# A hybrid state-space and convolution block on one core: a convolution split by parity, statistics and loads in another order, other paces

## The chip, the cores and the metric

The kernel runs on 1 core of one Trainium2 chip. The metric is device time in microseconds; before the change the median of 3 runs is 3039.42 us (3037.2 to 3045.06).

## The reference

One transformer-like block on x of 2048 tokens by 1024 channels, in float32. Cut to what matters:

```python
mod = silu(c) @ w_mod + b_mod                        # shifts, scales and gains, 6 x 1024
h = modulate(rmsnorm(x + pos), sh1, sc1)
p = h @ w_in                                         # 512 | 1024 | 1024 | 1024 | 1024 columns
y = s5_bidirectional(p[:, :512], context, ...)       # two linear scans over time
ya = gelu(y + d * u); ya = ya * sigmoid(ya @ w_glu)
vb = p[:, 512:1536] * sigmoid(p[:, 1536:2560])
vb = depthwise_conv(vb, dw_kernel, taps=31, padding=15) + dw_bias
vb = silu(layernorm(vb))
merged = sigmoid(g_a) * (ya @ w_proj_a) + sigmoid(g_b) * (vb @ w_proj_b)
x = x + g1 * (merged @ w_out)
x = x + g2 * (silu(h2 @ w_gate) * (h2 @ w_up)) @ w_down
return rmsnorm(x)
```

## The kernel before

Activations lie channel-major: a tile is 128 channels by 1024 tokens, and tokens go in two halves of 1024. Each matmul operand is split into a high and a low part (`split`, lines 192 to 196; weights in `wload`, lines 152 to 165), and each product is three matmuls of 128x128 by 512 columns: high by high, high by low, low by high. Everything larger than the on-chip memory goes through DRAM tensors whose names begin with `d_`.

The kernel is written as a foreground of matmul loops and a background of generators. After every three matmuls of a k step, `tick()` (lines 80 to 86) adds `RATE` credits, and background generators, in the order of their list, are stepped while the credit is positive; a generator yields what its step costs in credits, or a tuple with a number of ticks to wait. `dve()` takes credits off for VectorE's work in the foreground. `finish()` empties a generator at once. This sets the program order; each engine works its own queue in order, the building layer moves an instruction forward where its operands are ready, `high_priority()` moves it further, and `behind(ins, LAG)` ties a convolution pass to the LAG-th instruction before it on its engine.

The stages, in order, with the lines that the change and the steps touch:

- **Start** (`run`, lines 1547 to 1609). `mod_load` issues the loads of w_mod on SyncE's queue; `loads(k)` puts the load of x tile k-1 between them and, at the end, two weight tiles. `mod_first` multiplies c by w_mod; inside it `vectors()` (line 244) loads the small vectors and dw_kernel on ScalarE's queue and transposes them, and `stats(k)` takes the row statistics of x tiles 0 to 3 at k = 2 and of tiles 4 to 7 at k = 4 (`norm_stat`). Then `norm_first` turns, scales and splits the first 512 tokens of h, and `v_first` (line 860) makes the first gated tile of the convolution's input, four groups of 24 matmuls.
- **Projections, half 0** (lines 1632 to 1668): `v_pair`, `u` and `g_tile` (gate tiles d_g). In the background `build_prep` (line 468) and `build` prepare the state-space matrices, and `convolve` runs the convolution of half 0.
- **Convolution** (`conv`, line 904): for each of 8 channel tiles, a load of 1054 (or 1039) columns into a `cin` tile (2 buffers), a first product on ScalarE (line 917) into an `acc` tile (3 buffers, shared with others), 30 passes of multiply and add over the whole width on VectorE (line 919), a running sum over tiles (line 924), and a store of `acc` to d_cv on the POOL queue (line 925). `conv_edge` does the 15 columns at the seam; `conv_stat` takes mean and variance, `conv_apply` normalizes.
- **State-space stage** (lines 1676 to 1684), beside `v_pair` and 14 gate tiles of half 1.
- **Tail** (`tail`, line 1703). `stage_b` (line 975) is the gated branch: 4 preparing steps (yah, yal), 4 GLU tiles that end in zah and zal, 8 tiles of w_proj_a. Its two halves b0 and b1 come one after the other, with `chain` (conv_apply, then mod_rest and the convolution of half 1) in the background. `merge`, `out_proj` and the feed-forward part `ffn_s` follow for half 0, then the same for half 1. In `feed` (line 1739) `h2s_first`, `h2s_second` and `sums` prepare operands beside `out_proj` and the first four FFN products (lines 1369 to 1383); `weights_open` takes one `acc` and other tiles as weight buffers.

Of the kernel before, what the change touches and what calls it, by code (L numbers as in the profile page):

```python
# [19 lines left out]
N = 2048  # L20
# [8 lines left out]
RATE = (0.75, 0.7, 0.66, 0.61, 0.6, 0.9)  # L29
CREDIT = 3.0  # L30

W_BUILD, W_NORM, W_MOD = 4, 4, 20
W_IN, W_SWAP, W_OUT = 2, 6, 2
W_SUM = 4
LAG = 4

G_EARLY = 14
# [3 lines left out]
GAP_L, GAP_R = 1184, 2016  # L41


class Kernel:
# [146 lines left out]

    def split(self, full, hi, lo):
# [11 lines left out]
    def setup(self):  # L204
# [15 lines left out]
        self.d_vp = dt([8, 128, N], "d_vp")  # L220
# [23 lines left out]
    def vectors(self):  # L244
        nc, A, cp = self.nc, self.A, self.cp
        rows = self.t4(shape=(88, 128), name="vrows")
        r = 0
        self.vcol = {}
        for name in ("b_mod", "norm1_g", "norm2_g", "dw_bias", "conv_norm_g", "conv_norm_b"):
# [4 lines left out]
            r += n  # L254
        ps = self.ms([128, 88])
        nc.tensor.transpose(ps, rows, self.ident[0:88, 0:88])
# [4 lines left out]
        dwr = self.t4(shape=(31, 1024), name="dwr")  # L261
        nc.scalar.dma_start(dwr, A["dw_kernel"][0])
        ps = self.ms([128, 8, 31])
        for k in range(8):
            nc.tensor.transpose(ps[:, k, :], dwr[:, k * 128 : (k + 1) * 128], self.ident[0:31, 0:31])
        nc.vector.tensor_copy(self.dwk, ps)

# [3 lines left out]
        self.s2 = cp.tile([128, 8], F32, name="s2")  # L271

# [195 lines left out]
    def build_prep(self, bp, xq):  # L468
# [18 lines left out]
        Ct = bp.tile([128, 2, 32, 16], F32, name="Ct")  # L487
        for r, nme in enumerate(("ssm_c_re", "ssm_c_im")):
            Cr = xq("Craw", F32, (128, 4, 2, 64))
            for d in range(2):  # L490
# [5 lines left out]
            ps = self.ms([128, 512])  # L496
            for q in range(4):
                nc.tensor.transpose(ps[:, q * 128 : (q + 1) * 128], Cr[:, q].rearrange("k g p -> k (g p)"), self.ident)
            v.tensor_copy(Ct[:, r].rearrange("p a c -> p (a c)"), ps)
            yield (0,)  # L500
# [120 lines left out]
        Br = xq("Braw", F32, (128, 2, 32, 16))  # L621
        Bt = bp.tile([128, 2, 32, 16], F32, name="Bt")
        for r, nme in enumerate(("ssm_b_re", "ssm_b_im")):
            nc.scalar.dma_start(Br[:, r], A[nme][0].rearrange("d (r g) p c -> (g p) (d r) c", g=2))
# [235 lines left out]
    def v_first(self, ws):  # L860

        nc = self.nc
        ps = [self.mm(), self.mm()]
        for b in range(2):
            for p, w in zip(ps, ws):
                self.gemm(p, w, 0, *self.h[0], blocks=(b,))
# [962 lines left out]
```

## Time and profile before

| what | us |
|---|---|
| median of 3 runs | 3039.42 |
| the profiled execution | 3042.31 |
| its span, first to last instruction | 3040.5 |
| TensorE (PE) busy | 2890.9 |
| VectorE (DVE) busy | 2182.9 |
| ScalarE (ACT) busy | 1221.0 |
| mean granted TensorE clock | 0.975 |

The profile is one execution. A page gives busy times; other views of the same trace give groups of instructions, waits, a timeline, and busy times in chosen stretches. "PE" is TensorE, "DVE" VectorE, "ACT" ScalarE, "SP" SyncE; a "q" behind the name is the engine's queue of instructions that issue DMA. An idle time is put down to what ended it last.

### The profile page before, as it was taken

The numbers are of one execution on the slowest core, as the hardware profiler recorded it, in microseconds if no ns is written. First come the engines' busy times: TensorE is split into PE (matmuls) and PEld (weight loads), VectorE is DVE, ScalarE is ACT, GpSimd is POOL, SyncE is SP. The second block draws the span as 40 slices with busy tenths as digits, with TensorE's granted clock in tenths as the row PEclk, the third lists the DMA queues.
The fourth block names the chain that finished last, engine by engine and source line by source line (L and its number), as shares of the span: only waits on it lengthen the run. The fifth ranks groups of instructions, "written<-read, shape, count | busy, mean of one in ns | idle before, by whom it ended". The sixth has DMA issues, their size and how long they took to land. (4 is left out here: it accounts for less than half of the span.)

```text
span 3040.5 us, 34659 instructions
## 1 busy us (share of the span) xinstructions
PE 2890.9 (95%) x12747; PEld 2335.4 (77%) x12747; DVE 2182.9 (72%) x3296; ACT 1221.0 (40%) x1675; POOL 313.2 (10%) x480
## 2 busy tenths in 40 slices
PE   7989999998999989998899999989999899999998
PEld 3768777777888767876677887868787788888887
DVE  6489988899899477896878897866466744344446
ACT  4323344334343472123534444445324544444443
POOL 0111311100011000000000011000100000110110
PEclk9999999999999999999999999999999999999999
DMA  5344544533443566856554566463756544664553
GB/s 202 124 116 126 155 158 159 166 110 110 124 127 101 180 208 236 279 171 204 117 123 114 127 142 141 115 163 110 203 199 215 133 106 111 138 136 111 113 122 130
DMA packets 400009, 450.09 MB, mean 148 GB/s; under 512 B 34849, under 2 KB 318849, under 8 KB 399840
## 3 DMA queue, kind: packets, MB, share of 16 engines
q1 hardware_dynamic: 336224, 272.59, 28.9%
q0 software_dynamic: 50160, 170.55, 23.0%
q10 hardware_dynamic: 13456, 4.75, 0.7%
q8 instruction: 100, 1.64, 0.2%
q14 instruction: 69, 0.57, 0.1%
HBM read 280.42 MB, written 167.36 MB: 147 GB/s over the span
## 5 line engine op out<-in xcount | busy, mean ns | idle before, releaser
L919 DVE SCALAR_TENSOR_TENSOR acc<-cin,dwk,acc 128x1009 f32<-128x1009 f32 (+1 forms) x480 | 609.5, 1272 | 3.8
L183 PE MATMUL mm<-hh,hi 128*128 128x512 f32 x1152 | 480.6, 417 | 1.8 <-ACT hi L161 1.3
L183 PE MATMUL mm<-hh,lo 128*128 128x512 f32 x1152 | 457.2, 397 | 0.8 <-DVE lo L163 0.8
L183 PE MATMUL mm<-hl,hi 128*128 128x512 f32 x1152 | 456.4, 396 | 0.0
L1215 PE MATMUL mm<-ah,hi 128*128 128x512 f32 x704 | 277.1, 394 | 16.8 <-DVE fg L1380 13.5
L1215 PE MATMUL mm<-ah,lo 128*128 128x512 f32 x704 | 275.4, 392 | 3.4 <-DVE lo L1249 3.4
L161 ACT ACTIVATE hi<-raw 128x1024 fp32r<-128x1024 f32 x148 | 156.2, 1055 | 286.4 <-PE mm L183 249.2
L1215 PE MATMUL mm<-al,hi 128*128 128x512 f32 x704 | 267.9, 393 | 0.0
L183 PEld LDWEIGHTS mm<-hh,lo 128*128 128x128 f32 x1152 | 219.0, 190 | 49.8 <-DVE lo L163 1.7
L183 PEld LDWEIGHTS mm<-hh,hi 128*128 128x128 f32 x1152 | 219.8, 191 | 48.6 <-issue 2.2
L183 PEld LDWEIGHTS mm<-hl,hi 128*128 128x128 f32 x1152 | 219.8, 191 | 44.8 <-issue 0.6
L1457 POOL DMA_DIRECT2D d_x<-fd x152 | 129.1, 851 | 1069.1 <-ACT fd L1456 1063.3
L163 DVE TENSOR_TENSOR lo<-raw,hi 128x1024 fp32r<-128x1024 f32 x148 | 180.5, 1220 | 79.4 <-ACT hi L161 76.5
L1456 ACT ACTIVATE fd<-mm,mod 128x1024 f32<-128x1024 f32 x152 | 166.9, 1111 | 134.5 <-PE mm L1215 102.2
L1249 DVE TENSOR_TENSOR lo<-raw,hi 128x1024 fp32r<-128x1024 f32 x85 | 103.8, 1221 | 131.8 <-ACT hi L1246 130.5
L1249 DVE TENSOR_TENSOR lo<-ex,hi 128x1024 fp32r<-128x1024 f32 x83 | 101.4, 1221 | 108.0 <-ACT hi L1246 107.7
L1215 PEld LDWEIGHTS mm<-ah,hi 128*128 128x128 f32 x704 | 133.5, 190 | 47.5 <-DVE fg L1380 14.8
L1215 PEld LDWEIGHTS mm<-ah,lo 128*128 128x128 f32 x704 | 133.2, 189 | 32.5 <-DVE lo L1249 4.9
L1303 ACT ACTIVATE fg<-fg 128x512 f32<-128x512 f32 x80 | 50.6, 632 | 265.0 <-DVE fg L1306 265.0
L1215 PEld LDWEIGHTS mm<-al,hi 128*128 128x128 f32 x704 | 133.4, 190 | 28.0 <-issue 0.5
L183 PE MATMUL mm<-mgh,hi 128*128 128x512 f32 x256 | 101.4, 397 | 4.3 <-ACT mgh L195 2.0
L1215 PE MATMUL mm<-B22h,ex 128*128 128x512 f32 x320 | 105.3, 390 | 0.0
(490 smaller groups left out, 6146.3 us busy)
## 6 DMA issues: line engine op xcount, KB each, us to landing
d_x<-fd POOLq DMA_DIRECT2D x152, 512.0 KB, 9.2
raw<-in_w_in_dram SPq DMA_DIRECT2D x72, 512.0 KB
wm<-in_w_mod_dram SPq DMA_DIRECT2D x48, 512.0 KB
d_g<-gsig POOLq DMA_DIRECT2D x32, 512.0 KB, 4.0
raw<-in_w_out_dram SPq DMA_DIRECT2D x32, 512.0 KB
raw<-in_w_ffn_up_dram SPq DMA_DIRECT2D x28, 512.0 KB
raw<-in_w_ffn_down_dram SPq DMA_DIRECT2D x25, 512.0 KB
ex<-in_w_ffn_down_dram SPq DMA_DIRECT2D x23, 512.0 KB
```

The source lines that it names most:

```text
L161: nc.scalar.activation(hi, raw, AF.Copy)
L163: nc.vector.tensor_tensor(lo, raw, hi.bitcast(F32), op=OP.subtract)
L183: nc.tensor.matmul(ps[:, b * bw : (b + 1) * bw], wt[:, k, c0 : c0 + 128], mv[k][:, b * bw : (b + 1) * bw], start=(k == 0 and j == 0), stop ...
L919: self.behind(nc.vector.scalar_tensor_tensor(a, x[:, i : i + W], K(i), a, op0=OP.mult, op1=OP.add), LAG)
L1215: nc.tensor.matmul(ps, wt[:, k, c0 : c0 + 128], mv[k], start=start and k == 0 and j == passes[0], stop=stop and k == n - 1 and j == passes ...
L1249: i = nc.vector.tensor_tensor(lo, f, hi.bitcast(F32), op=OP.subtract)
L1303: self.last_act = nc.scalar.activation(o, i, f)
L1456: nc.scalar.activation(o, ps, AF.Copy, scale=mod)
L1457: nc.gpsimd.dma_start(self.d_x1[r, :, hs], o, accum_op=OP.add)
```

## The change

Numbers: `RATE` goes from (0.75, 0.7, 0.66, 0.61, 0.6, 0.9) to (0.75, 0.65, 0.61, 0.61, 0.6, 0.64), `W_MOD` from 20 to 12, `G_EARLY` from 14 to 12, and an unused gap of on-chip memory shrinks.

**Convolution.** The input d_vp is stored as even and odd columns apart (`[8, 128, 2, N // 2]`). With E and O the even and odd columns, one filter of 16 taps goes over E, one of 15 over O, and one of 16 taps (the pairwise sums of the taps, `dws`) over E + O; even outputs are the third less the first two, odd outputs the sum of the first two. Each runs over 512 columns. The results lie in the `cin` tile and are stored from there; half 1 keeps two fixed accumulators. The order of tokens in d_cv is by parity, and `merge` undoes it.

```diff
-        a = vp.tile([128, HALF], F32, tag="acc", name=self.nm("acc"), bufs=3)[:, 0:W]
+        a, b = accs or [vp.tile([128, HALF], F32, tag="acc", name=self.nm("acc"), bufs=3) for _ in range(2)]
+        p1, p2, q = a[:, 0:512], a[:, 512:1024], b[:, 0:512]
         K = lambda i: self.dwk[:, ft, i : i + 1]
-        nc.scalar.activation(a, x[:, 0:W], AF.Identity, scale=K(0), bias=self.V("dw_bias", ft))
-        for i in range(1, 31):
-            self.behind(nc.vector.scalar_tensor_tensor(a, x[:, i : i + W], K(i), a, op0=OP.mult, op1=OP.add), LAG)
-            yield 1.18
+        o = 1 if hf else 0
+        TS(p1, E[:, 0:512], K(0), None, op0=OP.mult)
+        TS(p2, O[:, o : o + 512], K(1), None, op0=OP.mult)
+        yield 0.8
+        for j in range(1, 16):
+            self.behind(STT(p1, E[:, j : j + 512], K(2 * j), p1, op0=OP.mult, op1=OP.add), LAG)
+            if j < 15:
+                self.behind(STT(p2, O[:, j + o : j + o + 512], K(2 * j + 1), p2, op0=OP.mult, op1=OP.add), LAG)
+            yield 1.2
+        TT(E, E, O, op=OP.add)
+        TS(q, E[:, 0:512], self.dws[:, ft, 0:1], None, op0=OP.mult)
+        yield 1.0
+        for j in range(1, 16):
+            self.behind(STT(q, E[:, j : j + 512], self.dws[:, ft, j : j + 1], q, op0=OP.mult, op1=OP.add), LAG)
+            yield 0.6
...
+        STT(q, q, bias, p1, op0=OP.add, op1=OP.subtract)
+        if hf == 0:
+            TT(ye, q, p2, op=OP.subtract)
+            STT(yo[:, 0:511], p1[:, 0:511], bias, p2[:, 1:512], op0=OP.add, op1=OP.add)
...
+        yield 1.8
...
-        nc.gpsimd.dma_start(self.d_cv[ft, :, hf * HALF : hf * HALF + W], a)
+        nc.gpsimd.dma_start(self.d_cv[ft, :, hf * HALF : (hf + 1) * HALF], y)
         yield 1.2
```

`conv_edge` takes 16 columns instead of 15 and writes them by parity. In `conv_stat` two loads of d_cv go ahead, half 1 waits six ticks before each step, and half 1 uses the convolution's two accumulators as mean and variance.

**Start.** `vectors_load()` issues the small vectors before `mod_load`; dw_kernel comes last on SyncE's queue and its transposes (`taps()`) after `v_first`; statistics of x tiles 4 to 7 leave `mod_first`, and `v_first`, now a generator over k with both weight tiles at each step, runs interleaved with `norm_first` and those statistics.

```diff
                 def loads(k):
                     if k == 8:
                         wr.extend(self.wraw(w) for w in wsrc)
-                    if k:
+                        self.norm_load(x, xt[4:8], nc.sync)
+                        self.dwr = self.t4(shape=(31, 1024), name="dwr")
+                        nc.sync.dma_start(self.dwr, A["dw_kernel"][0])
+                    elif 0 < k < 5:
                         self.norm_load(x, xt[k - 1 : k], nc.sync)
...
+                go = self.v_first(ws)
+                for k in range(8):
+                    for _ in range(5 if k == 0 else 2):
+                        next(first, None)
+                    next(second_stat, None)
+                    next(go)
```

In `build_prep` the loads of B follow those of C at once, and the transposes of C come after the scalar chain.

**Products.** `gemm_pair` works two output tiles together, all k steps but the last first; `stage_b` uses it for its first two w_proj_a tiles and `out_proj` for the first two of the first 512 tokens. In `ffn_s` the activation, product and split of the first four tiles get high priority.

```diff
+    def gemm_pair(self, pair, mhi, mlo, blocks=(0, 1)):
+        nc = self.nc
+        kt = len(mhi)
+        for ks in (range(kt - 1), (kt - 1,)):
+            for ps, (whi, wlo), c0 in pair:
+                for b in blocks:
+                    bs = slice(b * 512, (b + 1) * 512)
+                    for k in ks:
+                        for j, (wt, mv) in enumerate(((whi, mhi), (whi, mlo), (wlo, mhi))):
+                            nc.tensor.matmul(
...
```

**Gate tiles.** Tiles 12 and 13 of half 1 come beside b0's preparation, 14 and 15 in `tail`; the chain waits for the second.

```diff
         def chain(cv):
-            while cv in self.bgq:
+            while cv in self.bgq or not gates:
                 yield (2,)
...
         take(b0, 4)
+        self.g_tile(14, (1,))
         b1 = self.stage_b(1, "P", "P")
         e = self.bg(self.prep_b(b1))
         take(b0)
         self.finish(e)
+        take(b1, 4)
+        self.g_tile(15, (1,))
+        gates.append(True)
         take(b1)
```

## Rows read from the trace of the kernel before

**Rows 1.** Page, section 1: busy us (share of the span) and instructions.
```profile
PE 2890.9 (95%) x12747; PEld 2335.4 (77%) x12747; DVE 2182.9 (72%) x3296; ACT 1221.0 (40%) x1675; POOL 313.2 (10%) x480
```

**Rows 2.** Stretches: length, busy us of PE PEld DVE ACT POOL, clock, DMA, GB/s.
```profile
200.00:600.00 400.00, 386.49 (x1821) 311.61 (x1821) 365.39 (x585) 148.19 (x308) 82.47 (x146) 0.98 0.48 148
1075.00:1175.00 100.00, 86.36 (x334) 66.25 (x334) 72.22 (x65) 62.33 (x53) 4.25 (x8) 0.91 0.66 226
1475.00:1500.00 25.00, 15.89 (x59) 11.89 (x58) 22.99 (x36) 10.40 (x15) 2.60 (x3) 0.80 0.41 91
1575.00:1600.00 25.00, 20.13 (x77) 15.95 (x76) 13.84 (x15) 10.64 (x14) 0.84 (x1) 0.86 0.47 106
1825.00:1850.00 25.00, 20.25 (x83) 16.31 (x82) 15.02 (x16) 9.40 (x12) 0.84 (x1) 0.93 0.57 137
2000.00:2050.00 50.00, 41.65 (x166) 33.23 (x165) 31.17 (x33) 22.79 (x26) 5.21 (x7) 0.90 0.78 193
2375.00:2400.00 25.00, 17.18 (x72) 13.46 (x71) 24.91 (x40) 12.95 (x20) 0.00 (x0) 0.91 0.27 84
2450.00:2475.00 25.00, 25.00 (x112) 20.71 (x111) 11.97 (x15) 10.64 (x11) 3.69 (x5) 1.00 0.54 110
```

**Rows 3.** SyncE's queue, waits in 0 to 60 us: total, times, longest.
```profile
SPq L284 <- DMA dwr<-in_dw_kernel_dram: 9.0, 1, 9.0
```

**Rows 4.** Stretches of the start, columns as in rows 2.
```profile
20.00:25.00 5.00, 5.00 (x17) 1.31 (x15) 1.27 (x4) 0.00 (x0) 0.00 (x0) 0.68 0.25 65
30.00:35.00 5.00, 5.00 (x11) 0.99 (x9) 1.25 (x3) 1.14 (x3) 0.00 (x0) 0.65 1.02 406
```

**Rows 5.** Timeline of the start: start us, us, engine, line, operation, [idle before].
```profile
49.59 1.04 ACT L195 ACTIVATE mhi<-wm 128x1024 fp32r<-128x1024 f32 x1
...
61.69 0.77 PE L183 MATMUL mm<-hh,hi 128*128 128x512 f32 x1
```

**Rows 6.** Who TensorE waited for: us in total, times, longest.
```profile
PE ms L971 <- DVE dgr L969: 12.3, 4, 5.4
PE ms L668 <- DVE wr L659: 11.0, 1, 11.0
...
PE ms L1045 <- DVE vs L1040: 3.0, 1, 3.0
...
PE mm L183 <- ACT mgh L195: 2.0, 1, 2.0
```

**Rows 7.** VectorE by form: name, shapes, count, busy us, mean ns, idle before.
```profile
L919 DVE SCALAR_TENSOR_TENSOR acc<-cin,dwk,acc 128x1024 f32<-128x1024 f32 x240 | 306.4, 1279 | 1.8
...
L163 DVE TENSOR_TENSOR lo<-raw,hi 128x1024 fp32r<-128x1024 f32 x148 | 180.5, 1220 | 79.4 <-ACT hi L161 76.5 <-issue 2.3
...
L1306 DVE TENSOR_TENSOR fu<-fu,fg 128x512 f32<-128x512 f32 x40 | 27.6, 691 | 21.0 <-ACT fg L1303 21.0
...
L1109 DVE SCALAR_TENSOR_TENSOR xt<-mm,mod,xt 128x512 f32<-128x512 f32 x32 | 24.0, 749 | 35.0 <-PE mm L183 20.8 <-DMA xt<-d_xt 14.2
...
L1590 DVE TENSOR_SCALAR nrm<-x,ny 128x1024 f32<-128x1024 f32 x8 | 5.5, 747 | 0.1
```

**Rows 8.** ScalarE by form, columns as in rows 7.
```profile
L900 ACT ACTIVATE gsig<-mm 128x1024 f32<-128x1024 f32 x32 | 32.4, 1013 | 1.6 <-PE mm L183 1.4
...
L854 ACT ACTIVATE ut<-mm 128x1024 f32<-128x1024 f32 x8 | 8.1, 1017 | 5.1 <-PE mm L183 5.1
```

**Rows 9.** Stretch 950 to 1000, line 919 (convolution passes) alone.
```profile
950.00:1000.00 50.00, 22.86 (x18) 1.00 0.38 118
```

**Rows 10.** Timeline of TensorE, gated branch and first FFN tiles.
```profile
1146.92 1.22 PE L183 MATMUL mm<-yah,hi 128*128 128x512 f32 x2 [2.38 <-ACT yah L195]
...
1484.86 0.79 PE L1215 MATMUL mm<-ah,hi 128*128 128x512 f32 x1 [7.09 <-DVE fg L1380]
```

**Rows 11.** Timeline of ScalarE at the first product of a convolution tile.
```profile
1576.64 1.24 ACT L917 ACTIVATE acc<-cin,vec,dwk 128x1024 f32<-128x1024 f32 x1 [7.56 <-DMA d_cv<-acc]
```

**Rows 12.** Line 925, the stores of d_cv: from issue to landing.
```profile
DMA to landing us min/median/max: 3.3/6.3/11.0
```

More of the change, by code (lines that the diff above doesn't have):

```diff
@@ L242, in setup, with vectors_load @@
         nc.scalar.activation(self.sc.rearrange("p k w -> p w k"), ps, AF.Silu)
-    def vectors(self):
-        nc, A, cp = self.nc, self.A, self.cp
-        rows = self.t4(shape=(88, 128), name="vrows")
+    def vectors_load(self):
+        nc, A = self.nc, self.A
+        rows = self.vrows = self.t4(shape=(88, 128), name="vrows")
         r = 0
@@ L254, in vectors @@
             r += n
+    def vectors(self):
+        nc, cp = self.nc, self.cp
         ps = self.ms([128, 88])
-        nc.tensor.transpose(ps, rows, self.ident[0:88, 0:88])
+        nc.tensor.transpose(ps, self.vrows, self.ident[0:88, 0:88])
         self.vec = cp.tile([128, 88], F32, name="vec")
@@ L260, in vectors @@
         self.dwk = cp.tile([128, 8, 31], F32, name="dwk")
[L261 to L266, printed above, removed]
+        self.dws = cp.tile([128, 8, 16], F32, name="dws")
+        self.edge = cp.tile([128, 8], F32, name="edge")
         self.sh1 = cp.tile([128, 8, 2], F32, name="sh1")
@@ L495, in build_prep @@
             yield (0,)
[L496 to L500, printed above, removed]
+        Br = xq("Braw", F32, (128, 2, 32, 16))
+        for r, nme in enumerate(("ssm_b_re", "ssm_b_im")):
+            nc.scalar.dma_start(Br[:, r], A[nme][0].rearrange("d (r g) p c -> (g p) (d r) c", g=2))
         dsk = bp.tile([32, 16], F32, name="dsk")
@@ L1031, in conv_stat @@
         yield (6,)
+        cs = []
         for k in range(8):
-            c = self.cin.tile([128, HALF + 30], F32, tag="cin", name=self.nm("cvs"))[:, 0:HALF]
-            nc.sync.dma_start(c, self.d_cv[k, :, hs])
+            for i in (0, 1) if k == 0 else (k + 1,) if k < 7 else ():
+                cs.append(self.cin.tile([128, HALF + 30], F32, tag="cin", name=self.nm("cvs"))[:, 0:HALF])
+                nc.sync.dma_start(cs[i], self.d_cv[i, :, hs])
+            yield (6,) if hf else 0
+            c = cs[k]
             nc.vector.tensor_tensor(c, c, mean, op=OP.subtract)
@@ L1102, in out_proj @@
         rs = vp.tile([128, HALF], F32, tag="csum", name=self.nm("rs"))[:, 0:W]
-        for m in range(8):
-            w = self.wload(A["w_out"][0, :, m * 128 : (m + 1) * 128])
-            ps = self.mm()
-            self.gemm(ps, w, 0, *mg, blocks=blocks)
+        load = lambda m: self.wload(A["w_out"][0, :, m * 128 : (m + 1) * 128])
+        pair = []
+        if c0 == 0:
+            pair = [(self.mm(), load(m), 0) for m in range(2)]
+            self.gemm_pair(pair, *mg, blocks=blocks)
+        for m in range(8):
+            if m < len(pair):
+                ps = pair[m][0]
+            else:
+                w = load(m)
+                ps = self.mm()
+                self.gemm(ps, w, 0, *mg, blocks=blocks)
             xt = self.t4(name="xt")[:, 0:W]
@@ L1628, in run @@
                 self.vdone = False
-                self.v_first(ws)
+                go = self.v_first(ws)
+                for k in range(8):
+                    for _ in range(5 if k == 0 else 2):
+                        next(first, None)
+                    next(second_stat, None)
+                    next(go)
+                drain(first)
+                drain(second_stat)
+                scaled(1, nrm1, last)
+                ea = self.bg(self.norm_first(sp, nrm1, hh, hl, 512))
+                self.credit = 8.0
+                for _ in range(4):
+                    self.step(ea)
+                drain(go)
                 self.finish(ea)
+                self.taps()
                 eb = self.bg(early())
@@ L1718, in convolve @@
         def convolve():
-            for tok in self.conv_half(vp, 1, cs1):
+            accs = [vp.tile([128, HALF], F32, tag="acc", name=self.nm("acc"), bufs=3) for _ in range(2)]
+            for tok in self.conv_half(vp, 1, cs1, accs):
                 yield tok
```

166 lines of the change are left out of this document (115 added, 51 removed).

## The prediction

> **What bounds the kernel now.** I read the page first. TensorE is busy for 95% of the span [rows 1]; VectorE comes next, and where the convolution's first half runs beside the projections, from 200 to 600 us, it is busy 365 of 400 us without TensorE losing more than a little [rows 2]. So the change can only give back time that TensorE loses. That loss has two parts, and a table of stretches shows both at once: undisturbed, TensorE puts 112 matmuls into 25 us at clock 1.00 (last line of [rows 2]), 0.223 us each. [...] From these rows: 1075 to 1175 holds 334 of 448, 25.4 us lost; 1475 to 1500, 59: 11.8; 1575 to 1600, 77: 7.8; 1825 to 1850, 83: 6.5; 2000 to 2050, 166 of 224: 12.9; 2375 to 2400, 72: 8.9. That is 73 us, and it lies on stage borders, not in the long loops. The other large loss is the start: the first matmul of the input projection begins at 61.7 us [rows 5]. The third view is who TensorE waited for, the fourth VectorE's forms by cost.
>
> **The change part by part.** The profiled execution took 3042.3 us (span 3040.5 and 1.8 around it), 2.9 above the median of the runs shown, 3039.4. All sums are against 3042.3.
>
> *1. The start, -12.* The loads of w_mod are the stream that the first gate vectors wait for. SyncE's queue stood 9.0 us behind the load of dw_kernel, 31 rows issued on ScalarE's queue whose semaphore the next w_mod load shares [rows 3]; from 20 to 25 us the DMA engines are 25% busy at 65 GB/s, from 30 to 35 they move 406 GB/s [rows 4]. The change puts dw_kernel last on SyncE's queue, behind x tiles 4 to 7, which also leave the stream ahead of the last w_mod pieces: three of them, 1.57 MB at 406 GB/s, are 3.9 us; the hole is worth about 5 (0.75 of 5 us in that row and a piece before it). The last split on ScalarE starts at 49.6 [rows 5], behind statistics of tiles 4 to 7, which now come after it. So first matmul some 15 to 20 us earlier, near 44. It then runs at the pace of norm_first, and the second half of v_first waits for statistics that used to be ready; I put 5 us of that gain there, and take 12 of it, between -4 (the hole alone, partly refilled) and -18. What is queued behind dw_kernel on SyncE is the weight load of the second v_pair, needed 30 us later. The vrows loads only change place in ScalarE's queue: nothing.
>
> *2. Loads of B and C early, -2.* TensorE's transposes of wr stand 11.0 us [rows 6], because VectorE's products with Braw wait for its load. Braw is still issued behind 64 small C loads on the same queue, so I expect the wait mostly to move with the start. Ends: -16 (gone, with its low clock) and +5 (a longer C transpose).
>
> *3. The convolution's arithmetic, 0.* Per tile, before: 30 passes of 1.28 us and a sum of 1.22 (a 1024-column pass) [rows 7], about 39.5 us. After: 46 scalar_tensor_tensor of 512 columns. The nearest row reads PSUM and takes 0.749 [rows 7]: 34.4. Two additions at 0.69 [rows 7] are 1.4, three scalings about 0.46 (an estimate between nothing and the 0.747 of a 1024-column one [rows 7]) 1.4, the sum 1.2, small fills 0.2: 38.6 us. A quarter of the elements goes, but 52 instructions stand where 31 stood, and half the columns cost 0.59 of the time. Sixteen tiles save some 14 us on VectorE, which isn't the bound, and a 1.2 us step each on ScalarE. [...] What matters more: the pacing charges a tile 31.8 credits instead of 36.6, so a credit of convolution is 1.21 us of VectorE where it was 1.08, and RATE falls by only 7% in two stages and not at all in others. VectorE gets denser while half 0 runs; the waits for dgr behind its backlog are 12.3 us now [rows 6]. Ends: -5 and +20.
> Writing even and odd columns apart costs nothing on ScalarE: the strided PSUM read of ut takes 1017 ns, the plain one of gsig 1013 [rows 8].
>
> *4. Statistics of half 0, -6.* Half 0 of the convolution now needs 8 x 4.8 = 38 credits fewer; its last 18 passes of 240 lie after the state-space stage, at 950 to 1000 [rows 9], so it ends before that stage, and the statistics follow while gate tiles run. TensorE's 3.0 us wait for vs [rows 6] goes, and the low clock behind it (about as much). Ends -7 and 0.
>
> *5. Gated branch, -22.* Here 25.4 us are lost [rows 2]: TensorE waits for yah and zah (2.38 us in the first row [rows 10], one of seven such gaps), because conv_apply takes the credits and VectorE ahead of stage_b's preparation. The change holds conv_apply back until a gate tile has been put behind each half's GLU tiles. A gate tile is 48 matmuls, 10.7 us; the chain from a GLU tile's last matmul, two ScalarE passes of 1.0 [rows 8] and three VectorE passes of 1.2 [rows 7], is under 7. gemm_pair puts 36 matmuls (8.0 us) ahead of the first that needs the last zah. Ends -24 and -10.
>
> *6. What that pushes back, +8.* conv_apply (8 steps of three such passes, 3.7 us of VectorE) moves into b1's eight proj_a tiles, 43 us of TensorE, where VectorE also has 12 passes of 1.2: 44 us, full. Then mod_rest and its 28 loads run inside merge(0). I take a wait of 5 us at merge's first tile and 3 for the w_mod sums. Ends 0 and +20.
>
> *7. Pairs in out_proj, -4.* The wait for mgh, 2.0 [rows 6], and the low clock behind it. Ends -5 and 0.
>
> *8. First FFN tiles of each half, -18.* 11.8 and 8.9 us are lost [rows 2]. In the first, the product and split of the last tile stand in VectorE's queue among the sums, and TensorE waits 7.09 us for them [rows 10]. High priority puts them where the PSUM tile is ready; RATE 0.64 instead of 0.9 thins the work around them, and finish() may leave one step of h2s_second late (2 us). Ends -20 and -8.
>
> *9. Accumulators and ScalarE, -11; spread statistics of half 1, -7.* At 1576.6 ScalarE has stood 7.56 us at the first product of a later tile, which needs an accumulator whose store has not landed [rows 11]; fd and fg queue behind it, and TensorE loses 7.8; the same at 1828, 6.5. Now the product is VectorE's and nothing stores the accumulators, so -14.3 goes; but the result lies in the cin tile, whose next fills (VectorE) and loads (SyncE) wait for that store, so I take back 3. From 2000 to 2050 half 1's statistics load with no slack (12.9 lost); loading two ahead and spacing by six ticks should give back half. Ends for both: -26 and 0.
>
> Sum: -12 -2 +0 -6 -22 +8 -4 -18 -11 -7 = -74, so 3042.3 - 74 = 2968.
>
> **The rivals.** *A: half of the small gains don't come.* With VectorE denser, steps 3, 4 and 9 fail: +13 at the dgr waits, and -6 and -18 lost: 2968 + 37 = 3005. For it: VectorE is already busy 91% of the stretch from 200 to 600 [rows 2]; against: shorter passes let a priority instruction in after 0.75 us instead of 1.28.
>
> *B: half 1 of the convolution comes too late.* It now starts behind the held conv_apply and mod_rest. The FFN groups of half 0 give about 259 credits (28 ticks x 0.61 less 11.8 a group, 92 x 0.61 less 28.4 for two groups and a down unit); needed are 254, 21 for the statistics and about 15 lost in their waits, less some 31 earned earlier: 259, no slack. If those 31 don't come, 37 us of convolution, 20 of statistics, 6 of the row and 29 of conv_apply, 92 in all, stand against 43 us of down units: TensorE waits 45 or so, 3013.
>
> *C: slower.* The cin tile's fills on VectorE wait for d_cv to land, 3.3 to 11.0 us after issue, median 6.3 [rows 12], the wait moved from ScalarE to the busier engine, now for 12 tiles (six a half) instead of two or three. At 7.8 us of TensorE an event, the cost seen for such a wait [rows 2], 12 x 7.8 = 94, without the 11 of step 9: 2968 + 11 + 94 = 3073. It makes the change a loss from 5.3 us a tile (63 / 12). Against: the fills can come a whole tile after the store.
>
> *D: no change.* The gaps are replaced one for one, as in-order queues often do; 3042.
>
> **How the numbers follow.** The forecast has 0.57, A 0.20, B 0.12, D 0.05, C 0.06. Faster by over 0.3% (9 us, about what a measurement of this kernel can tell from no change) takes the first three, less a little: 0.88; same 0.05; slower 0.07. The range: the ends of steps 1, 5, 8 and 9 together on the good side are -24 beyond the sum with step 2's -14, so 2930; on the other side it reaches past B to 3016.
>
> **What would show it.** Right: the first L183 matmul near 44 us; the gated branch and the first FFN tiles at 105 or more matmuls in 25 us; no ScalarE wait on d_cv; convolution passes near 0.75 us; VectorE's busy sum within 20 us of before. Wrong: VectorE waiting on d_cv at the fills (C); TensorE idle after the down units of half 0 (B); longer waits on dgr (A).

## The result, and the profile after

The changed kernel takes 2966.4 us (median of 4 runs, 2964.0 to 2968.9) against 3038.3 for the kernel before on the same chip: a ratio of 0.976, 95% interval 0.974 to 0.978. The prediction was 2968. The profiled execution took 2964.0 us (span 2962.2). Run again beside the experiments, the same kernel took 2972.2 us for 3042.4, a ratio of 0.9775 (0.9762 to 0.9788); the experiments below are compared with that one (`after_again`).

The total came within 2 us in the first measurement and 4 in the second, but several of its terms did not: some that were counted gave nothing that can be told, and others that were put at little or nothing made up for them. That is the subject of what follows.

Page of the kernel after, section 1, columns as in [rows 1]:

```profile
PE 2864.2 (97%) x12747; PEld 2316.3 (78%) x12747; DVE 2142.5 (72%) x3673; ACT 1195.3 (40%) x1652; POOL 316.3 (11%) x481
```

VectorE runs 377 more instructions and is busy 40 us less; TensorE's busy time fell by 27 us with the same matmuls; its granted clock over the span is 0.987, before 0.975. The stretches, columns as in [rows 2]. The gated branch begins 55 us earlier, so the part of it that [rows 2] shows now lies at 1020 to 1120; the first FFN tiles of the two halves lie 45 and some 70 us earlier:

```profile
200.00:600.00 400.00, 388.42 (x1834) 312.42 (x1833) 376.78 (x757) 143.10 (x299) 81.32 (x141) 0.99 0.50 155
1020.00:1120.00 100.00, 94.49 (x416) 77.66 (x415) 52.16 (x54) 39.15 (x34) 4.79 (x9) 0.97 0.46 153
1425.00:1450.00 25.00, 25.00 (x111) 20.25 (x109) 20.89 (x34) 12.91 (x18) 5.16 (x6) 1.00 0.88 175
...
1925.00:1975.00 50.00, 41.13 (x164) 32.03 (x162) 34.33 (x38) 23.43 (x28) 4.82 (x6) 0.90 0.75 185
2320.00:2345.00 25.00, 24.21 (x105) 19.05 (x104) 18.64 (x29) 12.96 (x15) 6.01 (x8) 1.00 0.82 149
```

This part of the gated branch has 416 matmuls in 100 us where it had 334, the first FFN tiles 111 in 25 us for 59 and 105 for 72. The stretch with half 1's statistics is as thin as before (164 in 50 us, before 166; 172 in `after_again`). The whole gated branch, from its first matmul to the first of the merge, in the kernel before and then after:

```profile
1057.40:1222.30 164.90, 149.70 (x626) 117.81 (x626) 121.76 (x111) 80.41 (x70) 8.21 (x16) 0.94 0.65 223
```

```profile
1002.30:1172.30 170.00, 160.74 (x706) 131.79 (x705) 101.17 (x104) 74.43 (x66) 9.57 (x18) 0.97 0.56 189
```

The branch after holds two gate tiles more. At the prediction's 0.223 us a matmul, 739 and 762 would fit, so 25 us are lost in the branch before and some 12 after. Who TensorE waited for in the kernel after, columns as in [rows 6]:

```profile
PE ms L1064 <- DVE dgr L1062: 9.2, 4, 3.6
PE mm L1327 <- ACT fg L1415: 7.8, 5, 6.5
PE mm L1650 <- DMA ex<-d_x: 7.1, 1, 7.1
PE mm L183 <- DVE ga L1114: 5.5, 1, 5.5
PE ms L470 <- DVE s L358: 4.7, 1, 4.7
...
PE ms L697 <- DVE tw L601: 2.6, 1, 2.6
```

The 11.0 us ahead of wr and the 2.0 for mgh [rows 6] have shrunk or gone; new are 4.7 us for the gate vector s, 5.5 for ga, and a longer wait for ex (7.1, before 4.3).

Where the time went, by the start of each stage's first matmul (us). A spill transpose turns a tile of x that ScalarE then copies and the POOL queue stores to DRAM (d_xt).

| stage begins | before | after | after_again | after - before | gained or lost since the line above |
|---|---|---|---|---|---|
| first projection | 61.7 | 52.2 | 48.3 | -9.5 | -9.5 |
| first spill transpose | 90.5 | 91.4 | 86.1 | +0.9 | +10.4 |
| state-space stage | 624.7 | 609.2 | 608.1 | -15.5 | -16.4 |
| merge of half 0 | 1222.3 | 1172.3 | 1172.0 | -50.0 | -34.5 |
| first FFN tile, half 0 | 1420.7 | 1375.4 | 1375.7 | -45.3 | +4.7 |
| FFN groups, half 0 | 1512.5 | 1451.1 | 1454.4 | -61.4 | -16.1 |
| first transposes of the final norm | 2167.6 | 2094.2 | 2099.4 | -73.4 | -12.0 |
| end of the last full matmul | 3033.8 | 2955.5 | 2962.9 | -78.3 | -4.9 |

### The profile page after: what moved, and what is told of

The parts are those of the page before. It is cut to its first block, busy times and chain, and to the rows that moved or that the text cites. A ratio compares the mean times of both kernels' runs of the same rounds, so it can differ in the third digit from the quotient of the medians.

```text
span 2962.2 us, 35056 instructions
## 1 busy us (share of the span) xinstructions
PE 2864.2 (97%) x12747; PEld 2316.3 (78%) x12747; DVE 2142.5 (72%) x3673; ACT 1195.3 (40%) x1652; POOL 316.3 (11%) x481
## 4 chain that ended last, share of the span: by engine, by line
PE 42%; issue 37%; DVE 7%; DMA 7%; POOL 3%; ACT 2%; SPq 0%; ACTq 0%; POOLq 0%; DVEq 0%
PE mm L183 19%; PE mm L1327 17%; POOL d_x L1571 2%; PE ms L1327 2%; DMA d_in<-st 1%; DVE acc L985 1%; DVE lo L163 1%; PE ms L772 1%; DMA d_xt<-xts 1%; PE mm L899 1%; DVE acc L977 1%; DVE acc L979 1%; DMA pr<-in_posr_dram 0%; PE ms L837 0%; PE ms L838 0%
## 5 line engine op out<-in xcount | busy, mean ns | idle before, releaser
L183 PE MATMUL mm<-hh,hi 128*128 128x512 f32 x1120 | 462.9, 413 | 0.0
L183 PE MATMUL mm<-hl,hi 128*128 128x512 f32 x1120 | 441.3, 394 | 0.0
L183 PE MATMUL mm<-hh,lo 128*128 128x512 f32 x1120 | 440.8, 394 | 0.0
L183 PEld LDWEIGHTS mm<-hh,hi 128*128 128x128 f32 x1120 | 211.2, 189 | 44.5 <-issue 2.6
L183 PEld LDWEIGHTS mm<-hh,lo 128*128 128x128 f32 x1120 | 211.0, 188 | 44.6 <-issue 0.4
L183 PEld LDWEIGHTS mm<-hl,hi 128*128 128x128 f32 x1120 | 211.7, 189 | 43.2 <-issue 1.4
L163 DVE TENSOR_TENSOR lo<-raw,hi 128x1024 fp32r<-128x1024 f32 x148 | 180.3, 1220 | 64.5 <-ACT hi L161 60.6
L985 DVE SCALAR_TENSOR_TENSOR acc<-cin,dws,acc 128x512 f32<-128x512 f32 x240 | 179.2, 746 | 2.8
L977 DVE SCALAR_TENSOR_TENSOR acc<-cin,dwk,acc 128x512 f32<-128x512 f32 x240 | 178.1, 742 | 1.9 <-issue 1.7
L979 DVE SCALAR_TENSOR_TENSOR acc<-cin,dwk,acc 128x512 f32<-128x512 f32 x224 | 166.3, 742 | 0.3
```

What stands on the lines that cost most here:

```text
L163: nc.vector.tensor_tensor(lo, raw, hi.bitcast(F32), op=OP.subtract)
L183: nc.tensor.matmul(ps[:, b * bw : (b + 1) * bw], wt[:, k, c0 : c0 + 128], mv[k][:, b * bw : (b + 1) * bw], start=(k == 0 and j == 0), stop ...
L977: self.behind(STT(p1, E[:, j : j + 512], K(2 * j), p1, op0=OP.mult, op1=OP.add), LAG)
L979: self.behind(STT(p2, O[:, j + o : j + o + 512], K(2 * j + 1), p2, op0=OP.mult, op1=OP.add), LAG)
L985: self.behind(STT(q, E[:, j : j + 512], self.dws[:, ft, j : j + 1], q, op0=OP.mult, op1=OP.add), LAG)
```

## The experiments

A cost in us below is the difference of a run's ratio from 0.9775, times 3042. Where the intervals of two ratios overlap it isn't told apart from nothing.

**How far two runs can be told apart: `after_again`.** The kernel after itself.

> The kernel after, unchanged, beside the others on their chip. The kernel with the first FFN tiles as before has the same instructions up to 1370 us, and yet its state-space stage begins 8.9 us later in its profile than in the profile of after. Theory: this part of the program (C transposes, wr, dgr) varies by that much from run to run, so the state-space stage begins between 609 and 619 us here and the time is 2964 to 2973. Rival: that profile was of a disturbed run, and this one begins the stage within 2 us of 609 and takes 2964 to 2969.

2972.2 us, where the theory had it; the state-space stage begins at 608.1, where the rival had it. The other runs decide: `ffn_old`, `gates_old`, `pair_old`, `stat1_old` and `prep_final` below have the same instructions up to that stage and begin it at 618.0, 615.8, 612.7, 611.8 and 611.0. One stretch, kernel after and then `ffn_old`, columns as in [rows 2]:

```profile
91.00:609.00 518.00, 496.84 (x2345) 397.63 (x2346) 459.05 (x1020) 176.45 (x360) 100.95 (x174) 0.99 0.51 154
```

```profile
91.00:609.00 518.00, 489.66 (x2287) 392.18 (x2286) 446.64 (x1002) 170.79 (x354) 100.70 (x174) 0.98 0.50 150
```

58 matmuls, 13 us, differ in the same program: the small waits come out a few us longer or shorter (over after, `gates_old`, `pair_old` and `stat1_old` 1.1 to 6.4 us for wr and 8.3 to 11.9 for dgr), and TensorE's granted clock stands at 0.50 for 6.8 us of this stretch in the first and 23.8 in the second. So a stage reading of under some 10 us ahead of 620 us decides nothing by itself; later stages are read by their own length.

**The start: `start_old`.** The order of loads, the statistics and the first pair as before; dw_kernel on ScalarE's queue again:

```diff
-    self.norm_load(x, xt[4:8], nc.sync)
-    self.dwr = ...; nc.sync.dma_start(self.dwr, A["dw_kernel"][0])
-elif 0 < k < 5:
+if k:
     self.norm_load(x, xt[k - 1 : k], nc.sync)
...
+    if k == 4:
+        drain(self.norm_stat(sp, xt[4:8], True, rs, posr))
```

> The kernel after with its start put back: x tiles one by one between the w_mod loads, dw_kernel on ScalarE's queue ahead of its transposes, statistics of tiles 4 to 7 before the last gate vectors, the first projection pair in one piece. Theory: the new start brings its gate vectors forward but loses that again before the spills (TensorE stands 4.7 us for the vector s, then runs 13.6 us at half clock), so undoing it costs nothing: 2960 to 2970 us, although the last matmul of w_mod comes some 11 us later. Rival (the prediction's first step, a gain of 12 that lasts): 2978. In either case everything after 100 us should look as in the kernel after.

2973.7 us, ratio 0.978 (0.976 to 0.980): 1 us over after_again, nothing. (The range expected, up to 2970, was set against the 2966 of the first measurement.) Its first projection begins at 59.6, its first spill at 88.2, its state-space stage at 608.2. The new start's lead is gone by the spills, and these rows of the kernel after's timeline (columns as in [rows 5]; VectorE, SyncE, TensorE) show how:

```profile
49.06 0.69 DVE L407 TENSOR_TENSOR x<-x,posc 128x512 f32<-128x512 f32 x1 [3.69 <-DMA x<-in_x_dram]
49.67 0.17 DVE L354 TENSOR_TENSOR s<-ms,vec 128x16 f32<-128x16 f32 x1
50.29 0.69 DVE L407 TENSOR_TENSOR x<-x,posc 128x512 f32<-128x512 f32 x1 [0.45 <-DMA x<-in_x_dram]
...
51.09 0.17 DVE L358 SCALAR_TENSOR_TENSOR s<-s,vec 128x16 f32<-128x16 f32 x1
...
40.70 2.75 SPq L170 DMA_DIRECT2D raw<-in_w_in_dram  x2
43.50 1.05 SPq L388 DMA_DIRECT2D x<-in_x_dram  x2
...
51.29 1.09 PE L470 MATMUL ms<-ident,nrm 128*128 128x128 f32 x4 [4.73 <-DVE s L358]
```

On VectorE the addition of the position to a late x tile stands in front of the arithmetic of s; its load was issued at 43.5, behind two weight loads. TensorE, done with the transposes of the gate rows at 46.1, waits to 51.3; its granted clock stands at 0.50 from 46.8 to 60.4.

**Is that the whole reason? `vec_order`.** The additions are ordered behind s:

```diff
-second_stat = self.norm_stat(sp, xt[4:8], True, rs, posr)
+second_stat = self.norm_stat(sp, xt[4:8], True, rs, posr, last)
...
+    if after and i < 4:
+        self.order(add, after)
```

> The kernel after with one order added: the additions of the position to x tiles 4 to 7 stand on VectorE behind the arithmetic of the gate vectors s. Theory: in the kernel after these additions wait for their loads (6.8 us in all) in front of s, so s comes at 51 us although its transposes end at 46; with the order s should come near 47 us, the first projection matmul near 48 instead of 52, the stretch at half clock should start 4 us earlier or be shorter, and the time fall by 4 to 10 us, to 2956 to 2962. Rival: the start is bound by the loads of x tiles 4 to 7 themselves, so the wait only moves to the statistics and the second half of the normalisation: 2964 to 2968.

Half of this theory held: the wait for s is gone, the first projection begins at 43.4 (the time the prediction named) and the spills at 82.6, 8.8 us earlier than in after. The time didn't follow: 2977.7 us, above both ranges, ratio 0.979 (0.977 to 0.981), not told apart from after. (The profiled execution is the slowest of its four, 2983.5.) Half of the lead is gone at wr, where TensorE waits 6.5 us, and all of it at the state-space stage, which begins at 611.6 (columns as in [rows 6]; TensorE, then VectorE):

```profile
PE ms L699 <- DVE tw L603: 6.5, 1, 6.5
...
DVE Bt L658 <- DMA Braw<-in_ssm_b_re_dram: 6.3, 1, 6.3
```

VectorE's product with B waits for its load 6.3 us, against 2.3 in after. Against after, the lead is 8.8 us at the spills, 8.5 at the issue of the first load of C (99.0 for 107.5), 6.0 at that of B (146.4 for 152.4), 3.9 at the product with B (157.4 for 161.3) and 4.1 at wr (166.9 for 171.0). In the kernels whose load of B follows those of C in the program the transposes of wr begin between 166.6 and 171.5 us, although their first projection begins anywhere from 43.4 to 59.6. So what the start wins is taken back on the way to the next thing that is late, the loads of C and B, which ScalarE's queue issues one by one for some 45 us. That these loads are the whole reason isn't shown.

**The load of B: `bload_old`.** In the program its issue goes back behind the C transposes, and these go back into the loop of the C loads:

```diff
-Br = xq("Braw", ...); nc.scalar.dma_start(Br[:, r], ...)     # ahead of build_prep's arithmetic
+Br = xq("Braw", ...); nc.scalar.dma_start(Br[:, r], ...)     # ahead of the products with it
```

> The kernel after with the loads of B issued where they were, behind the C transposes, and the C transposes inside the load loop. Theory (step 2, corrected by the profile of after): the wait before the transposes of wr, 2.6 us in after, becomes 9 to 12 again and the two C waits shorten by 1 to 2; some of it is given back by 600 us, where the profiles of other kernels showed that such leads are lost: 2966 to 2974. Rival (the early B load is the whole gain of 16 us between 91 and 600): 2980 or more.

2980.6 us, ratio 0.9795 (0.9781 to 0.9809): 6 us dearer by the medians, but the intervals overlap. TensorE's wait, columns as in [rows 6]:

```profile
PE ms L696 <- DVE wr L687: 11.2, 1, 11.2
```

It is the 11.0 us of [rows 6] again, so this edit made the wait go. What that is worth isn't settled: the time lies above the theory's range and in the rival's, and the state-space stage begins at 617.2, inside the 608 to 618 of the unchanged program. Nor is the load issued any earlier in the kernel after. The issues of B in after, then in `bload_old` (columns as in [rows 5]; ScalarE's queue):

```profile
152.37 0.47 ACTq L526 DMA_DIRECT2D Braw<-in_ssm_b_re_dram  x1
```

```profile
149.69 0.45 ACTq L652 DMA_DIRECT2D Braw<-in_ssm_b_re_dram  x1
```

In both it stands directly behind the last load of C, as it does in the kernel before (153.7). What differs is the time from this issue to VectorE's first product with B: 8.9 us in after and 9.1 in `after_again`, 15.9 in `bload_old` and 15.6 before. Why the load is ready sooner stays open.

**The arithmetic: `conv_old_dve`, and the first product on ScalarE: `conv_old`.** The convolution of before, 31 passes of 1024 columns with the result stored from one of three rotating accumulators, at the pace of after (31.8 credits a tile). The first has the first product on VectorE, the second on ScalarE:

```diff
-TS(p1, E[:, 0:512], K(0), None, op0=OP.mult) ... 44 passes of 512, sums, q
+nc.vector.tensor_scalar(a, x[:, 0:W], K(0), bias, op0=OP.mult, op1=OP.add)     # conv_old_dve
+nc.scalar.activation(a, x[:, 0:W], AF.Identity, scale=K(0), bias=bias)         # conv_old
+for i in range(1, 31):
+    STT(a, x[:, i : i + W], K(i), a, op0=OP.mult, op1=OP.add)
+    yield 1.02
...
+nc.gpsimd.dma_start(self.d_cv[...], a)
```

> The kernel after with the convolution's arithmetic of before (31 passes of 1024 columns, the first one on VectorE, the result stored from one of three rotating accumulators, plain order of columns), at the credits a tile of after (31.8), so that the pace is the same. Theory (step 3): the arithmetic itself is worth nothing on the path, although VectorE is busy some 30 us longer: 2964 to 2974, with the same gaps as the kernel after. Rival: passes of 1.28 us hold back VectorE's urgent work (dgr, gating products, splits) by half a microsecond more each, and the time is 2980 to 2995.

> As the kernel with the old arithmetic (conv_old_dve), but with the first product of each tile on ScalarE, as in the kernel before. Theory (step 9): ScalarE stands 5 to 8 us at some first products in the second half, waiting for an accumulator whose store is under way, its gating passes queue behind, and TensorE loses 8 to 14 us against the run with VectorE's product. Rival: the stall came from the old pace; within 3 us of the run with VectorE's product.

With VectorE's product 2987.8 us, ratio 0.982 (0.981 to 0.984): the arithmetic and what hangs on it are worth 15 us, where step 3 had 0. The rival's range was right; its mechanism, that VectorE's urgent work is held back by half a microsecond a pass, isn't shown. With ScalarE's product 2999.7, ratio 0.987 (0.985 to 0.990): another 15 us, where step 9 had 11. Here the mechanism is in plain view. Waits of ScalarE in `conv_old`, of VectorE in `conv_old_dve`, both from 1390 to 2130 us, columns as in [rows 6]:

```profile
ACT acc L959 <- DMA d_cv<-acc: 24.8, 5, 6.9
```

```profile
DVE acc L959 <- DMA d_cv<-acc: 4.1, 2, 3.3
```

and one of the five in the timeline of `conv_old` (ScalarE, then TensorE):

```profile
1544.41 1.24 ACT L959 ACTIVATE acc<-cin,vec,dwk 128x1024 f32<-128x1024 f32 x1 [6.86 <-DMA d_cv<-acc]
1545.56 0.58 ACT L1363 ACTIVATE fu<-mm 128x512 f32<-128x512 f32 x1
...
1548.14 0.79 PE L1275 MATMUL mm<-T3h,hi 128*128 128x512 f32 x1 [4.80 <-ACT fg L1363]
```

It is [rows 11] again: the product waits for a store, FFN copies queue behind it, TensorE stands 4.8 us. In the kernel after ScalarE has no wait on d_cv. The wait for the store has moved to SyncE's queue, ahead of the loads into the cin tiles:

```profile
SPq L966 <- DMA d_cv<-cin: 45.1, 4, 20.0
...
SPq L961 <- DMA d_cv<-cin: 24.8, 4, 9.8
```

70 us of waiting in eight places, and no gap of TensorE's is released by a cin tile. VectorE, in whose queue the prediction's rival C put this wait, waited for the cin tiles' loads 10.8 us in two places, both at the first tile of a half (104 and 1176 us), and never for a store of d_cv.

**The first FFN tiles: `ffn_old`.**

```diff
-    with self.tc.high_priority():
-        nc.vector.tensor_tensor(g, ps, g, op=OP.mult)
-        self.split(g, ...)
+    nc.vector.tensor_tensor(g, ps, g, op=OP.mult)
+    self.split(g, ...)
...
-RATE = (..., 0.6, 0.64)
+RATE = (..., 0.6, 0.9)
```

> The kernel after with the first FFN tiles as before: no priority for the gating product and its split, and the pace of that stage at 0.9 instead of 0.64. Theory (step 8): TensorE waits some 7 and 6 us for the last tile's product again, in both halves, with the low clock behind it: 2978 to 2986. Rival: the shorter passes of the convolution alone let the product through in time, so the time stays within 2962 to 2970.

2991.2 us, ratio 0.984 (0.982 to 0.986): 19 us dearer, 5 above the expected range. The two stretches of `ffn_old`, columns as in [rows 2]:

```profile
1425.00:1450.00 25.00, 19.36 (x75) 15.14 (x74) 25.00 (x40) 10.56 (x16) 0.00 (x0) 0.86 0.36 110
2325.00:2350.00 25.00, 17.18 (x65) 13.19 (x64) 24.12 (x39) 11.43 (x17) 0.87 (x1) 0.80 0.35 97
```

75 and 65 matmuls where after has 111 and 105, with VectorE full: the product stands among the sums again (gaps of 5.6 and 6.1 us before ah). By their own length the two stages from the first FFN tile to the FFN groups account for 12 us, 84.6 and 81.9 us for 78.7 and 75.8 in after_again. The profiled run also begins its state-space stage 10 us later, ahead of anything that the edit touches, so the 19 may be partly that.

**The gate tiles: `gates_old`.** All gate tiles ahead of the gated branch, conv_apply not held:

```diff
-G_EARLY = 12
+G_EARLY = 14
...
-while cv in self.bgq or not gates:
+while cv in self.bgq:
...
-self.g_tile(14, (1,)) ... take(b1, 4); self.g_tile(15, (1,)); gates.append(True)
```

> The kernel after without the two held back gate tiles: all gate tiles run ahead of the gated branch and the application of the convolution isn't held. Theory (steps 5 and 6 of the prediction, 22 gained and 8 given back): the waits for yah and zah come back at 1030 to 1130 us and the waits at the merge's first tile go, so 2974 to 2986. Rival: the gain of the gated branch comes from the pace and the shorter passes, and the gate tiles only change place: 2962 to 2970.

2974.2 us, ratio 0.978 (0.976 to 0.980): nothing, so step 5's 22 less 8 are not there at the end. In the stage they are. Columns as in [rows 2]:

```profile
1060.00:1160.00 100.00, 90.36 (x374) 71.63 (x374) 76.12 (x73) 55.50 (x47) 4.78 (x9) 0.95 0.71 235
```

374 matmuls for 416 in the same part of the branch, with 4.8 us of waits for yah; from the state-space stage to the merge `gates_old` takes 581.1 us, after_again 563.9. Then it gets them back, 19 us in all: 7 by the first FFN tile, 5 more by the groups of half 0, 4 inside the groups, and 3 by the end. Its second half of the convolution starts earlier, and the statistics of half 1 end at 1963 instead of 2014. So the gate tiles move a loss from the gated branch to later stages; that the later convolution is the reason is argued, not tested.

**The pairs: `pair_old`, and the spaced statistics: `stat1_old`.**

```diff
-pair = [(self.mm(), w, mm * 128) for mm in range(2)] if m2 == 0 else None     # pair_old; out_proj's too
+pair = None
...
-for i in (0, 1) if k == 0 else (k + 1,) if k < 7 else ():                     # stat1_old
+for i in (k,):
...
-    yield (6,) if hf else 0
```

> The kernel after without the paired products, in proj_a and in out_proj. Theory: in proj_a the pair hid the wait for the last GLU tile, but in after TensorE stands 5.5 us at the fourth proj tile, because the product that frees its PSUM tile is on VectorE behind splits of the next half that wait for ScalarE; without the pair that wait gets smaller by at most 1 us and the waits for zah (about 2 us) and mgh (about 2 us) come back, with low clock behind them: 2974 to 2980. Rival: the pair itself makes the 5.5 us, since it ends two PSUM tiles at nearly one time; then it goes, and the time is 2962 to 2970.

> The kernel after with the statistics of the convolution loading one tile at a time and without the six ticks between the tiles of half 1. Theory (second part of step 9): the stretch behind the second half's last convolution tile (1930 to 1960 us in after, where TensorE still stands 2.3 and 4 to 6.5 us) gets 3 to 8 us longer, and the time 2975 to 2980 against 2972 for after. Rival: those waits are of the same size either way, since the gating product there waits for ScalarE and not for the statistics: 2968 to 2974.

2972.9 us (ratio 0.977, 0.975 to 0.980) and 2970.1 (0.976, 0.974 to 0.978): neither is worth anything that these runs can tell. For the pairs both ranges were missed; for the statistics the rival's was right. The 5.5 us wait for ga is there without the pairs too (5.4), so the pair doesn't make it. Beside half 1's statistics TensorE waits for the gating product fg either way (6.5 us in after, 4.1 in after_again, 2.5 in `stat1_old`), and the stretch is no thinner without the spacing. `stat1_old`, columns as in [rows 2]:

```profile
1925.00:1975.00 50.00, 44.79 (x178) 34.83 (x177) 36.79 (x43) 22.89 (x25) 7.37 (x9) 0.93 0.83 195
```

**Do the gains add? `three_old`.** The edits of conv_old, ffn_old and bload_old together.

> The kernel after with the three groups undone together that cost most when undone alone: the convolution's arithmetic with its first product on ScalarE (conv_old, 27.5 us over after's 2972.2), the first FFN tiles (ffn_old, 19.0) and the loads of B (bload_old, 8.4). Theory: the gains add, and the start, the held gate tiles, the pairs, the pace and the spaced statistics are together worth what is left: 2972 + 55 = 3027, within 6, which leaves 15 us to the kernel before. Rival 1: the three groups are all of the gain, since the undone parts make each other worse (the FFN's waits with a slower convolution beside them): 3036 to 3044. Rival 2: they overlap, each partly the same waits: 3005 to 3018.

3024.6 us, ratio 0.995 (0.993 to 0.996): 52 us dearer than after, by the sum of the three 55. They add. 16 us are left to the kernel before for everything else: start, gate tiles, pairs, spaced statistics, and the pace, which wasn't undone alone. Undone one at a time the first four are worth nothing that these runs can tell. The stages say where the 16 us are won: `three_old` begins the state-space stage at 623.2, only 1.5 us ahead of the kernel before, and the merge of half 0 at 1190.7, 31.6 ahead; 9 of that are lost again by the end. One piece is a wait in the state-space stage of the kernel before that the prediction doesn't count (columns as in [rows 6]):

```profile
PE ms L808 <- ACT S L800: 8.5, 1, 8.5
```

It comes at 702 us, and TensorE's granted clock stands at 0.50 from 695.7 to 705.9. In `three_old` TensorE waits 1.1 us there, and in the other changed kernels 1.3 or less. The kernel before has one profile, and no run isolates which edit removes this wait.

**A better version: `prep_final`.** Two waits of the kernel after were new or longer, for ga and for ex:

```diff
-e = self.bg(self.prep_b(b1))
+take(b0, 2)
+e = self.bg(self.prep_b(b1))
 take(b0)
...
 if j < 0:
-    yield (16,)
+    yield (32,)
```

> The kernel after with two orders changed: the preparation of the second half's gated branch starts behind the first two proj tiles, and the first transposes of the final normalisation stand 32 ticks instead of 16 behind their loads. Theory: the 5.5 us wait at the fourth proj tile and the 7 to 8 us wait for the loads of ex go, each with some 7 to 10 us at half clock behind it: 8 to 18 us, so 2954 to 2964 against 2972 for after. Rival: the preparation comes too late and TensorE waits for the second half's GLU inputs instead, and the final transposes only push the same wait to the first FFN tiles: 2968 to 2976.

2962.5 us, ratio 0.974 (0.972 to 0.977), 10 us below after_again; the intervals of the two ratios just overlap, so the medians alone would not settle it, but the stretch does. After_again and then `prep_final`, columns as in [rows 2]:

```profile
2080.00:2160.00 80.00, 72.16 (x336) 60.01 (x336) 46.86 (x113) 20.97 (x28) 12.83 (x17) 0.94 0.76 237
```

```profile
2080.00:2160.00 80.00, 80.00 (x387) 66.89 (x386) 52.55 (x129) 22.52 (x30) 12.80 (x18) 1.00 0.81 258
```

51 more matmuls, 11 us: TensorE's wait for ex, 7.8 us in after_again, is gone, since the transposes now stand far enough behind the loads of ex. From the merge of half 1 to its out_proj `prep_final` takes 95.4 us; the kernel after and the ten variants of it above take 99.2 to 106.4. The other edit failed. The first two products ga come at once, but the third is again behind a split of yal that waits for ScalarE, and the gap moved from 1067 to 1080 us:

```profile
1073.95 1.23 DVE L215 TENSOR_TENSOR yal<-yf,yah 128x1024 fp32r<-128x1024 f32 x1 [3.82 <-ACT yah L214]
1075.09 1.22 DVE L163 TENSOR_TENSOR lo<-raw,hi 128x1024 fp32r<-128x1024 f32 x1
1077.85 1.23 DVE L215 TENSOR_TENSOR yal<-yf,yah 128x1024 fp32r<-128x1024 f32 x1 [1.54 <-ACT yah L214]
1079.00 1.22 DVE L1114 TENSOR_TENSOR ga<-mm,ga 128x1024 f32<-128x1024 f32 x1
```

## Why the prediction was right, and where it wasn't

The two parts of the loss that the prediction reads from [rows 2] are idle time and low clock; a count of missing matmuls holds both. The low clock that steps 2, 4 and 7 count behind a wait is in the trace of the kernel before a granted clock of 0.50: from 170.0 to 180.3 us at the wait for wr, which ends at 176.5, from 1043.8 to 1054.1 at that for vs, which ends at 1044.8, and from 1327.1 to 1330.5 at that for mgh, which ends at 1327.4.

*1, start: -12 forecast, 0 measured.* The mechanism on the DMA queues was right (the last w_mod matmul ends near 42 us, 11 earlier), but the step "I put 5 us of that gain there" named too small a price and in the wrong place: the wait for the late x tiles falls on s itself, and 13.6 us at a granted clock of 0.50 stand behind it. `vec_order` takes that wait away, and the lead still isn't there at the state-space stage.

*2, loads of B: -2 forecast, about -6 measured, not told apart from nothing.* "I expect the wait mostly to move" failed: TensorE's wait fell from 11.0 to 2.6 us, and to 1.1 to 6.4 in the other runs with the same instructions up to there. The premise behind it, that B is still issued behind the C loads, holds.

*3, arithmetic: 0 forecast, about -15 measured,* outside its own ends (-5 and +20). Two parts of the step failed. The sum of durations fell by 15.5 us, close to the 14 forecast, but VectorE's busy time by 40, because passes overlap (0.66 us apart at 0.74 each, last section); the bound "busy sum within 20 us of before" was wrong with it. And "which isn't the bound" led to pricing only harm. Where the 15 us sit is not settled: the stages of `conv_old_dve` lose 8 us up to the state-space stage, 3 in it, and some 5 in the FFN groups, each within or near what one program varies by.

*4 and 5, statistics and gated branch: -28 forecast.* Half 0 of the convolution did end early, its last pass at 624.5 us, but the wait for vs stayed (2.4 us for 3.0). In the branch itself the loss fell from 25 us to 12, not to some 3: the waits for yah and zah went, the one for ga came. From the state-space stage to the merge the kernel after is 34.5 us shorter, but the change's own share that `gates_old` isolates is 17, and it is given back afterwards. The step that failed is the sum: it took a stage's gain for the program's.

*6, pushed back work: +8 forecast.* From the merge to the first FFN tile of half 0 the kernel after lost 4.7, pairs included, and took 6 to 7 more than `gates_old`: the price was about right for these stages, but more than 10 us are handed back behind them. *7, pairs: -4 forecast, 0 measured.* *8, first FFN tiles: -18 forecast, -19 by the ratio, -12 in the two stages.* *9, accumulators: -11 forecast, -15 measured; spaced statistics: -7 forecast, 0 measured.*

So for arithmetic, accumulators, FFN tiles and B the forecast had -31, and 52 were measured with all undone together; for everything else it had -43, and 16 are left. The two errors, 21 and 27, nearly cancel: that the total came so close is luck, while steps 8 and 9 (accumulators) were right in mechanism and nearly in size.

*Rivals.* A's headline came true in size and not by its mechanism: 37 us of the gains counted didn't come, but they were those of the start, the gate tiles, the pairs and the spaced statistics, and the waits for dgr didn't get longer (9.2 us for 12.3). B didn't come: half 1's statistics end at 2014, before the down units of half 0 are done. C's wait came, but in SyncE's queue, and no gap of TensorE's was traced to it. D is excluded by the interval. Of the signs named, no ScalarE wait on d_cv and passes near 0.75 us came; the first projection near 44 us came only in `vec_order`, and the branch is just under 105 matmuls in 25 us.

One slip in the range: the ends of steps 1, 5, 8 and 9 lie 18 us beyond the sum, not 24, so its lower end follows as 2936. And of the 18 passes of [rows 9], 12 lie inside the state-space stage, whose last matmul ends at 976.3. Neither moves the sum.

## What to carry to other kernels

A gain at a stage border counts only if what is due next isn't late already: check the next load or the next VectorE chain before adding it to the sum, since here a start 9 us earlier and a stretch around the gated branch 17 us shorter were both worth nothing at the end. A wait that can't be avoided should stand in the queue of the engine that nobody waits for: with the wait for a store on ScalarE the kernel took 15 us more than with it on VectorE (24.8 us of waits for 4.1), and 70 us of such waits on SyncE ended no gap of TensorE's. Where a transpose waits for a load that is issued late, more distance in the program order is a cheap repair (11 us here). And a total that comes out right says little about its terms: undo them one at a time, and some together.

## What the runs showed of the hardware

Two of VectorE's passes overlap in these rows where the next one doesn't read what the last one wrote, by some 0.07 us. The kernel after alternates between two accumulators in one part of the convolution and runs on one in the other (timeline, columns as in [rows 5]):

```profile
603.03 0.73 DVE L979 SCALAR_TENSOR_TENSOR acc<-cin,dwk,acc 128x512 f32<-128x512 f32 x1
603.70 0.73 DVE L977 SCALAR_TENSOR_TENSOR acc<-cin,dwk,acc 128x512 f32<-128x512 f32 x1
604.36 0.74 DVE L979 SCALAR_TENSOR_TENSOR acc<-cin,dwk,acc 128x512 f32<-128x512 f32 x1
605.02 0.74 DVE L977 SCALAR_TENSOR_TENSOR acc<-cin,dwk,acc 128x512 f32<-128x512 f32 x1
...
613.49 11.78 DVE L985 SCALAR_TENSOR_TENSOR acc<-cin,dws,acc 128x512 f32<-128x512 f32 x15
```

Alternating passes start 0.66 us apart, though each lasts 0.74; fifteen on one accumulator take 11.78, 0.785 each. The passes of before, all on one accumulator:

```profile
610.71 10.41 DVE L919 SCALAR_TENSOR_TENSOR acc<-cin,dwk,acc 128x1009 f32<-128x1009 f32 x8
```

1.30 each, for a duration of 1.265. So a half-length pass costs 0.51 of a full one where it alternates, not the 0.59 that step 3 took from the durations. The rows give the two sizes: 0.785 us a pass where it reads the last result, 0.66 where it doesn't. That the reading is the reason wasn't tested by an edit.

One and the same program differs by 13 us between 91 and 609 us from run to run (2345 and 2287 matmuls in that stretch), with waits of 1 to 6 us for wr and 6.8 and 23.8 us at a granted clock of 0.50; over seven profiles of it the next stage begins between 608.1 and 618.0.
